# An urgency rank in the planner, recurrences recorded ahead of the heads, the norm factor in the rotary tables, and softmax and projection work moved from VectorE to ScalarE

## Chip, cores and metric

One core of a Trainium2 chip runs the whole program in one launch. The metric is the device time in microseconds (us) of that core, the median of repeated runs; lower is better. The engines are TensorE (PE), VectorE (DVE), ScalarE (ACT), GpSimd (POOL), and SyncE (SP), which issues the transfers.

## The reference

Two transformer blocks follow each other on 512 latent tokens of width 1024, in fp32. The first also has 256 context tokens. Cut to what matters:

```python
# block 1: swiglu FFN, then token mixing (retention and gated linear attention, "GLA"), then swiglu FFN
x = x + 0.5 * m_l[2] * swiglu(modulate(rms_norm(x)), ffn1_w1, ffn1_w3, ffn1_w2)   # ctx likewise
x = x + m_l[5] * token_mixing(modulate(rms_norm(x)), modulate(rms_norm(ctx)), w_in, ...)
x = x + 0.5 * m_l[8] * swiglu(modulate(rms_norm(x)), ffn2_w1, ffn2_w3, ffn2_w2)
# block 2
xn = rmsnorm(h, norm_mix_g)
q, k, v, u, y = split(xn @ w_in_2)               # 512 columns each
q, k = rope(q, positions), rope(k, positions)
attn = dilated_mixture_attention(q, k, v)        # 8 heads of 64, mixture over three dilations
uc = centred_depthwise_conv(u, conv_w, conv_b)
rec = bidirectional_rglru(uc, ...) * gelu(y)     # r, i = sigmoid(...); linear recurrence, both ways
h = h + concatenate([attn, rec]) @ w_out_2
h = h + memory_cross_attention(rmsnorm(h), rmsnorm(mem), ...)
h = h + square(relu(rmsnorm(h) @ w_mlp_in)) @ w_mlp_out
return rmsnorm(h, norm_final_g)
```

## The kernel before

Activations lie feature-major, as tiles of 128 features by 512 tokens. Each fp32 factor is split into a high and a low part in fp32r (`pair`, `split`; weights in `wload`: `wh` is made by ScalarE, `wl` by VectorE), and a product is three matmuls: high by high, low by high, high by low. A sum of products lies in one of the 8 PSUM banks (tag `ps`; tiles `p` for projections, `as`, `at`, `ao` in attention). `MOST` limits how many banks some kinds may hold at a time, so `as` and `at` have two each.

The program records every operation with `Engine` and `Plan.add`. `Plan.issue()` then decides the order on each engine: it walks a model of time with a cost for each operation, and from the operations whose inputs are ready it takes the one that can start first. Among those that can start at the same moment it takes the one that was recorded first (`pick`). On VectorE and ScalarE an operation that was recorded earlier is also taken if it would start a little later (`YIELD`); on ScalarE `pick` stays with the activation table that is loaded, up to a limit. Each engine then runs its list strictly in that order. All operations are recorded through one helper, so the profile gives them all one line, L365, and the tiles' names tell them apart.

The change touches mainly block 2's mixer, at 1380 to 1640 us:

- `heads(i)` projects q and k of two heads, scales them (`fac` is `mix1`, the norm factor), rotates them (`rotated`: `sw` is a copy with swapped rows, by a transfer, then three VectorE operations with the tables `pcos` and `psin`), and splits them (`aqh`, `aql`, `akh`, `akl`).
- `attend(hp)` is the attention of these two heads, as 8 rows (2 heads by 4 tiles `i` of 128 queries). In each row the scores `as` come from two matmuls, VectorE adds the log counts and takes the extreme (`asm`, `mx`), ScalarE takes the exponential with its sum (`dn`), VectorE takes the reciprocal and scales the row, PE transposes it in four pieces (`at`), and ScalarE copies it out (`pt`). Then 64 matmuls of half a tile make `ao`.
- `convolve(i)` makes `uc`, `recur(i, j)` the recurrence for two tiles of it in both directions (all `rg_` tiles, chains on VectorE), and `gated(i)` the gate: `gy` is the y projection scaled by `fac`, then its gelu, then times `rec`.
- The projection `w2_out` sums over attention outputs and gated recurrences (`mix[0..7]`). It is the last user of all of them.

In token mixing (block 1), GpSimd makes some `lo` halves and copies of 64x64 pieces (`pg<-pd`) for GLA. `go` is a sum of GLA outputs on PE, `ro` one of retention.

Of the kernel before, what the change touches and what calls it, by code (L numbers as in the profile page):

```python
# [2 lines left out]

# [36 lines left out]
GROWN = 3  # L40

MOST = {"as": 2, "at": 2, "gl": 2, "gs": 2, "gx": 2, "rs": 2, "cs": 2, "ctp": 2, "rgr": 2, "rgi": 2}
LEVELS = (1, 2, 4, 8, 16, 32)

VEC = {}
# [99 lines left out]
class Plan:  # L145
# [9 lines left out]
    YIELD = 0.3  # L155

    def __init__(self, tc):
        self.tc, self.ops, self.caps, self.warm = tc, [], {}, False

    def engine(self, name, engine):  # L160
        return Engine(self, name, engine)
# [42 lines left out]
    def cost(self, name, method, args, kwargs, outs, ins):  # L204
        def cols(x):
            return int(np.prod(x.shape[1:]))

        if name == "PE":
            n = cols(args[0])
            rhs = args[2] if method == "matmul" else args[1]  # L210
            if method == "matmul" and rhs.tile.dtype == F32R and n >= 256:
                self.warm = True
                return 0.422 * n
            part = 1 if args[0].shape[0] != 64 else 0.75 if n == 64 else 0.53
            if method == "transpose":
                part = 0.5
            return part * max(1.69 * n * (1 if self.warm else 2), 213.0 if n < 64 else 107.0)
        if name == "SP":
            x = outs[0] if outs else ins[0]
            return int(np.prod(x.shape)) * 4 / 360.0 + 50  # L220
        n = max(cols(x) for x in outs)
        if name == "ACT":
            return 93 + 0.833 * n + 93 * sum(isinstance(kwargs.get(k), View) for k in ("bias", "scale", "accum_out"))
        if name == "POOL":
            return 150 + 2.1 * n
        if method == "reciprocal":
            return 60 + 6.3 * n
        if method == "tensor_tensor_reduce":
            return 330 + 1.04 * n
        pointers = sum(isinstance(x, View) and x.shape == (128, 1) for x in args[1:])  # L230
        fast = method in ("tensor_copy", "tensor_scalar", "memset") and not any(x.tile.key[0] == "pp" for x in ins)
        return 66 + (0.53 if fast else 1.04) * n + 60 * pointers

    def issue(self):
        ops, n = self.ops, len(self.ops)
# [26 lines left out]
        left = {t: t.left for t in seen}  # L262
        ahead = {}
        oldest, done = 0, [False] * n
        start, best, stale = [0.0] * n, {}, set(engines)
        order = []

# [17 lines left out]
        def pick(e):  # L285
            t0, choice = None, None
            cand = []
            for i in avail[e]:
                if i > oldest + self.WINDOW:
                    continue  # L290
                w = allowed(i)
                if w is not None:
                    cand.append((max(ready[i], w, clock[e]), i))
            if not cand:
                return None
            first = min(c[0] for c in cand)
            if e in ("DVE", "ACT"):

                i = min(c[1] for c in cand if c[0] <= first + 1.0)
                soon = [c for c in cand if c[1] < i and c[0] - first <= self.YIELD * ops[i][7]]  # L300
                if soon:
                    first = min(soon, key=lambda c: c[1])[0]
            now = [c for c in cand if c[0] <= first + 1.0]
            if e == "ACT":
                stay = [c for c in now if ops[c[1]][8] is None or table in ops[c[1]][8]]
                old = min(now, key=lambda c: c[1])
                if stay and not (first - ready[old[1]] > self.PATIENCE):
                    now = stay
            c = min(now, key=lambda c: c[1])
            return c  # L310

        while oldest < n:
# [65 lines left out]
def tile_two_blocks(ctx: ExitStack, tc: tile.TileContext, a: dict, out: bass.AP, dbg=None):  # L378
# [94 lines left out]
    def wwide(ap):  # L473

        return wcols(wload(ap[:, :1024]), 4, 256) + wcols(wload(ap[:, 1024:]), 4, 256)
# [407 lines left out]
        dump(f"c1_{k}", ctx_.x[k])  # L883


    hl_, hc_ = lat.h, ctx_.h


# [15 lines left out]
    def fm(ap, with_ctx, evac):  # L904

        w = wcols(wload(ap))
        ps = [bank()] + ([bank()[:, :NC]] if with_ctx else [])
        if leading[0] > 0:
            leading[0] -= 1
            two = [ps[0], bank()]  # L910
            for i, span in enumerate(((0, 256), (256, 512))):
                gemm([two[i][:, :256]], w, [cutp(lat.h, *span)])
                evac(slice(*span), two[i][:, :256])
            if with_ctx:
                gemm([ps[1]], w, [ctx_.h])
                evac(None, ps[1])
            return
        gemm(ps, w, [lat.h] + ([ctx_.h] if with_ctx else []))
        evac(slice(0, 512), ps[0])
        if with_ctx:  # L920
            evac(None, ps[1])
# [443 lines left out]
    V.tensor_scalar(ang, ang, lim, -lim, op0=ALU.min, op1=ALU.max)  # L1365
    S_.activation(pcos, n_, AF.Sin)
    S_.activation(psin, ang, AF.Sin)
    V.tensor_scalar(psin, psin, sgn, None, op0=ALU.mult)


    aq, ak = [None] * 4, [None] * 4
# [6 lines left out]
    def heads(i):  # L1378


        def parts(w, scale, name):
            x, hi, lo = slot(name + "t"), slotr(name + "h"), slotr(name + "l")
            fm(w, False, lambda _, pl: V.scalar_tensor_tensor(x, pl, scale, mix1, op0=ALU.mult, op1=ALU.mult))
            rotated(x, x, pcos, psin)
            S_.activation(hi, x, AF.Copy)
            V.tensor_sub(lo, x, hi.bitcast(F32))
            return hi, slotr(name + "s"), lo

        h0, h1, lo = parts(a["w2_q"][i], 0.125, "aq")
        sync.dma_start(h1[high].bitcast(F32), h0[high].bitcast(F32))  # L1390
        sync.dma_start(h1[low].bitcast(F32), lo[high].bitcast(F32))
        sync.dma_start(h0[high].bitcast(F32), lo[low].bitcast(F32))
        aq[i] = h0, h1
        h0, h1, lo = parts(a["w2_k"][i], 1.0, "ak")
        sync.dma_start(h1[high].bitcast(F32), h0[high].bitcast(F32))
        for one, two in ((h0, h1), (lo, slotr("akm"))):
            if one is lo:
                sync.dma_start(two[high].bitcast(F32), one[high].bitcast(F32))
            sync.dma_start(two[low].bitcast(F32), one[high].bitcast(F32))
            sync.dma_start(one[high].bitcast(F32), one[low].bitcast(F32))  # L1400
        ak[i] = (h0, h1), (lo, two)

    heads(0)
    for u in range(2):
        w = wwide(a["w2_v"][u])
        for t in range(4):
            po = bank()[:, :256]
            tok_major(w, lat.h, t, po)
            S_.activation(av[t][:, u * 256 : (u + 1) * 256], po, AF.Copy, scale=mixf[:, t : t + 1])


    sp8, sp4 = small(8, "sp8"), small(8, "sp4")
# [22 lines left out]
    def attend(hp):  # L1435
        pt = []
        for hh in range(2):
            for i in range(4):
                ps = bank("as")
                q, (k, lo) = aq[hp][hh][:, i * P : (i + 1) * P], ak[hp]  # L1440
                T.matmul(ps, q, k[hh], start=True, stop=False)
                T.matmul(ps, q, lo[hh], start=False, stop=True)
                sm = slot("asm")
                mx = plan.tile(tp, [P, 1], F32, "mx", fresh("mx"), 4)
                dn = plan.tile(tp, [P, 1], F32, "dn", fresh("dn"), 4)

                V.tensor_tensor_reduce(sm, ps, lnc[i], -1.0, 3.0e38, ALU.add, ALU.min, accum_out=mx)
                S_.activation(sm, sm, AF.Exp, scale=-1.0, bias=mx, accum_out=dn)
                V.reciprocal(dn, dn)
                V.tensor_scalar(sm, sm, dn, None, op0=ALU.mult)  # L1450
                pq = bank("at")
                for j in range(4):
                    T.transpose(pq[:, j * P : (j + 1) * P], sm[:, j * P : (j + 1) * P], ident)
                pt.append(slot("pt"))
                S_.activation(pt[-1], pq, AF.Copy)
        po = bank("ao")
        for i in range(4):
            for j in range(4):
                for hh in range(2):
                    h = 2 * hp + hh  # L1460
                    T.matmul(po[64 * hh : 64 * hh + 64, i * P : (i + 1) * P], av[j][:, h * 64 : h * 64 + 64],
                             pt[4 * hh + i][:, j * P : (j + 1) * P], start=(j == 0), stop=(j == 3))
        o = slot("aov")
        S_.activation(o, po, AF.Copy)
        dump(f"attn_{hp}", o)
        mix[hp] = pair(o)
# [40 lines left out]
    def gated(i):  # L1507
# [4 lines left out]
        dump(f"rec_{i}", gy)  # L1512
        mix[4 + i] = pair(gy)

    convolve(0)
    convolve(1)
    recur(0, 1)
    heads(1)  # L1520
    attend(0)
    heads(2)
    convolve(2)
    convolve(3)
    attend(1)
    recur(2, 3)
    gated(0)
    gated(1)
    heads(3)
    attend(2)  # L1530
    gated(2)
    gated(3)
    attend(3)
    lat.x = xt = [slot("x") for _ in range(NK)]
    for k in range(NK):
# [237 lines left out]
```

## Time and profile before

| | before |
|---|---|
| median of 3 runs | 2069.81 us (2064.95 to 2073.78) |
| the profiled execution | 2069.04 us, span 2067.3 us |
| mean granted TensorE clock | 0.984 |
| busy in the span | PE 1991.3 us, DVE 1203.4, ACT 795.1, POOL 49.3 |

The span is the time from the first to the last instruction; the rest of an execution's time lies around it. PE's idle time is 76 us, the difference between span and busy time.

### The profile page before, as it was taken

To read this page: it belongs to the slowest core of one execution; us is meant where nothing else is said; L and a number is where in the kernel's file an instruction comes from. 1 tells how busy PE (TensorE), PEld (TensorE's weight loads), DVE (VectorE), ACT (ScalarE), POOL (GpSimd) and SP (SyncE) were. 2 spreads that over 40 slices of the span, in tenths; PEclk is the share of its full clock that TensorE was granted. 3 is DMA by queue.
4 is the path that set the end of the run, shared out by engine and by line. 5 is a ranking of instruction groups with operands and counts; after the bars stand their busy time and mean duration, and the time that the engine had idled before them with its cause. 6 is when DMAs were issued, how large, how long until landed. Compare 5 with 4: busy or idle time off the path is not lost.

```text
span 2067.3 us, 27811 instructions
## 1 busy us (share of the span) xinstructions
PE 1991.3 (96%) x11033; PEld 1686.7 (82%) x11033; DVE 1203.4 (58%) x2221; ACT 795.1 (38%) x1239; POOL 49.3 (2%) x62
## 2 busy tenths in 40 slices
PE   5899999999999998999999999999987999999998
PEld 4879888888888876988988888888765888888887
DVE  7887844426247777589733333376977575343344
ACT  6452121221225654365332222245666463233241
POOL 0000000000000023110000000000000000000000
PEclk9989999999999999999999999999998999999999
DMA  8876624416132112232233333235242214333321
GB/s 314 274 234 199 198 76 137 147 63 218 58 107 88 53 52 72 67 92 75 85 117 92 119 93 103 83 102 161 57 137 55 62 52 135 100 94 100 94 70 41
DMA packets 76801, 231.33 MB, mean 112 GB/s; under 512 B 9808, under 2 KB 12544, under 8 KB 76672
## 3 DMA queue, kind: packets, MB, share of 16 engines
q1 hardware_dynamic: 76672, 229.57, 35.4%
q8 instruction: 86, 1.41, 0.3%
q14 instruction: 43, 0.35, 0.1%
HBM read 212.10 MB, written 7.34 MB: 106 GB/s over the span
## 4 chain that ended last, share of the span: by engine, by line
PE 90%; DVE 5%; ACT 2%; DMA 2%; issue 1%; POOL 0%; SPq 0%; DVEq 0%; ACTq 0%; POOLq 0%
PE p L365 81%; PE gs L365 1%; PE ro L365 1%; PE rs L365 1%; PE at L365 1%; PE st L365 1%; PE go L365 1%; DVE junk L365 1%; DMA wr<-in_ffn_up_dram 1%; PE ao L365 1%; PE gl L365 1%; PE as L365 1%; PE rb L365 0%; DVE rg_r L365 0%; PE co L365 0%
## 5 line engine op out<-in xcount | busy, mean ns | idle before, releaser
L365 ACT ACTIVATE wh<-wr 128x1024 fp32r<-128x1024 f32 (+4 forms) x295 | 298.1, 1013 | 751.8 <-PE p L365 581.0
L365 PE MATMUL p<-hh,wh 128*128 128x512 f32 (+1 forms) x1320 | 505.9, 390 | 12.8 <-ACT hh L365 7.3
L365 PE MATMUL p<-hl,wh 128*128 128x512 f32 (+1 forms) x1320 | 508.3, 389 | 0.0
L365 DVE TENSOR_TENSOR wl<-wr,wh 128x1024 fp32r<-128x1024 f32 (+4 forms) x295 | 343.0, 1168 | 168.6 <-ACT wh L365 78.1
L365 PE MATMUL p<-hh,wl 128*128 128x512 f32 (+1 forms) x1320 | 362.2, 387 | 3.9 <-DVE wl L365 3.9
L365 PE MATMUL p<-hi,wh 128*128 128x512 f32 (+1 forms) x831 | 307.3, 377 | 9.7 <-DVE gy L365 9.7
L365 PE MATMUL p<-lo,wh 128*128 128x512 f32 (+1 forms) x831 | 308.1, 377 | 0.0
L365 PEld LDWEIGHTS p<-hh,wh 128*128 128x128 f32 x1320 | 249.7, 190 | 55.9 <-ACT hh L365 9.3
L365 PEld LDWEIGHTS p<-hh,wl 128*128 128x128 f32 x1320 | 243.9, 190 | 52.6 <-DVE wl L365 4.3
L365 PEld LDWEIGHTS p<-hl,wh 128*128 128x128 f32 x1320 | 251.7, 191 | 37.4 <-issue 0.7
L365 PE MATMUL p<-hi,wl 128*128 128x512 f32 (+1 forms) x831 | 216.0, 376 | 0.0
L365 PEld LDWEIGHTS p<-hi,wh 128*128 128x128 f32 x831 | 156.9, 189 | 32.9 <-DVE gy L365 10.1
L365 PEld LDWEIGHTS p<-lo,wh 128*128 128x128 f32 x831 | 157.4, 189 | 21.1 <-issue 0.2
L365 PEld LDWEIGHTS p<-hi,wl 128*128 128x128 f32 x831 | 149.4, 189 | 27.6 <-issue 0.3
L365 PEld LDWEIGHTS p<-h,wh 128*128 128x128 f32 x816 | 138.8, 189 | 26.1
L365 DVE CUSTOM_DVE_ANT_0 junk<-wr,cond,vec 128x1024 f32<-128x1024 f32 x112 | 143.3, 1280 | 21.6 <-DMA wr<-in_ada_w_dram 20.8
L365 PE MATMUL p<-h,wh 128*128 128x256 f32 x816 | 145.5, 280 | 0.0
L365 DVE TENSOR_TENSOR act<-act,p 128x512 f32<-128x512 f32 (+1 forms) x68 | 38.3, 583 | 177.6 <-PE p L365 176.2
L365 DVE SCALAR_TENSOR_TENSOR x<-p,gate,x 128x512 f32<-128x512 f32 (+1 forms) x59 | 42.6, 723 | 106.2 <-PE p L365 106.1
L365 DVE TENSOR_TENSOR x<-p,x 128x512 f32<-128x512 f32 (+1 forms) x51 | 33.6, 659 | 115.8 <-PE p L365 115.7
L365 PE MATMUL p<-h,wl 128*128 128x256 f32 x408 | 97.3, 279 | 0.0
L365 PEld LDWEIGHTS p<-hid,wh 128*128 128x128 f32 x352 | 64.3, 188 | 14.3
(344 smaller groups left out, 2367.4 us busy)
## 6 DMA issues: line engine op xcount, KB each, us to landing
wr<-in_ffn_up_dram SPq DMA_DIRECT2D x100, 512.0 KB, 3.7
wr<-in_ada_w_dram SPq DMA_DIRECT2D x88, 512.0 KB, 4.4
wr<-in_mlp_up_dram SPq DMA_DIRECT2D x32, 512.0 KB, 3.6
wr<-in_mlp_dn_dram SPq DMA_DIRECT2D x32, 512.0 KB, 3.5
wr<-in_w_out_dram SPq DMA_DIRECT2D x16, 512.0 KB, 3.7
wr<-in_ffn_dn_dram SPq DMA_DIRECT2D x16, 448.0 KB, 3.2
wr<-in_ffn_dn_dram SPq DMA_DIRECT2D x16, 384.0 KB, 3.2
wr<-in_ffn_dn_dram SPq DMA_DIRECT2D x16, 320.0 KB, 2.9
```

The costliest lines, as they stand in the source:

```text
L365: ins = getattr(engine, method)(*args, **kwargs).ins
```

## The change

`Plan.issue` gets a rank. The new `latest` schedules the recorded operations backwards from the end of the program, and the later an operation may begin in that schedule, the later its rank. Operations recorded ahead of `plan.mark`, which stands between the first FFN and token mixing, keep their record order. `pick` uses the rank wherever it used the record index. The planner's cost of a fp32r matmul changes from 0.422n to 13 + 0.418n ns.

In block 2, the two recurrences are recorded ahead of most of the heads, and the V projections (`values`) behind `heads(0)` and `convolve(3)`. The factor `mix1` is multiplied into `pcos` and `psin` once. The eight evacuations of q and k, which multiplied by it on VectorE, become ScalarE copies with a constant scale. In `attend`, the rows with even `i` (16 of 32) are scaled by ScalarE.

```diff
 MOST = {"as": 2, "at": 2, ...}
+LOOK = 12
...
             if method == "matmul" and rhs.tile.dtype == F32R and n >= 256:
-                return 0.422 * n
+                return 13 + 0.418 * n
...
+    def latest(self, after):
+        ops, n = self.ops, len(self.ops)
+        left = [len(x) for x in after]
+        engines = sorted({o[0] for o in ops})
+        clock, heaps, begin = dict.fromkeys(engines, 0.0), {e: [] for e in engines}, [0.0] * n
+        due = [0.0] * n
...
+        for _ in range(n):
+            best = None
+            for e in engines:
+                near = heapq.nsmallest(LOOK, heaps[e])
+                for j in near:
+                    at = max(clock[e], due[-j])
+                    if best is None or (at, j) < best[:2]:
+                        best = at, j, e
...
+            name, cost = ops[i][0], ops[i][7]
+            clock[e] = begin[i] = at + cost
+            for d in ops[i][5]:
+                f = ops[d][0]
+                hop = (0 if f in ("SP", "PE") else self.CHAIN) if f == name else self.HOPS.get((f, name), self.HOP)
+                due[d] = max(due[d], begin[i] + hop + (2000 if f == "SP" else 0))
...
+        return [(0, i) if i < self.mark else (1, -x) for i, x in enumerate(begin)]
...
-            c = min(now, key=lambda c: c[1])
+            c = min(now, key=lambda c: rank[c[1]])
...
+    plan.mark = len(plan.ops)
     hl_, hc_ = lat.h, ctx_.h
...
-    V.tensor_scalar(psin, psin, sgn, None, op0=ALU.mult)
+    V.scalar_tensor_tensor(psin, psin, sgn, mix1, op0=ALU.mult, op1=ALU.mult)
+    V.tensor_mul(pcos, pcos, mix1)
...
-            fm(w, False, lambda _, pl: V.scalar_tensor_tensor(x, pl, scale, mix1, op0=ALU.mult, op1=ALU.mult))
+            fm(w, False, lambda _, pl: S_.activation(x, pl, AF.Copy, scale=scale))
...
-                V.tensor_scalar(sm, sm, dn, None, op0=ALU.mult)
+                if i % 2:
+                    V.tensor_scalar(sm, sm, dn, None, op0=ALU.mult)
+                else:
+                    S_.activation(sm, sm, AF.Copy, scale=dn)
...
     convolve(0)
     convolve(1)
     recur(0, 1)
+    convolve(2)
+    heads(0)
+    convolve(3)
+    values()
+    recur(2, 3)
     heads(1)
     attend(0)
-    heads(2)
-    convolve(2)
-    convolve(3)
-    attend(1)
-    recur(2, 3)
     gated(0)
     gated(1)
+    heads(2)
+    attend(1)
+    gated(2)
+    gated(3)
     heads(3)
     attend(2)
-    gated(2)
-    gated(3)
     attend(3)
```

(The old record began with `heads(0)` and the V projections, ahead of `convolve(0)`.)

The rank moves instructions on every engine behind the first FFN. Three places follow. The first is VectorE in the mixer at the end of `recur(2, 3)`, where the gate's evacuations (`gy<-p`), those of `heads(3)` (`aqt`, `akt`) and the first row of `attend(2)` (ISA, `as_2474`) stand. Before:

```order
L365 SCALAR_TENSOR_TENSOR rg_r_2430_13380<-rg_a_2432_13495,rg_r_2430_13380 128x512
L365 TENSOR_TENSOR rg_i_2431_13389<-rg_i_2431_13389,rg_r_2430_13380 128x512
L365 SCALAR_TENSOR_TENSOR rg_r_2430_13380<-rg_a_2432_13495,rg_i_2431_13389 128x512
L365 TENSOR_TENSOR rg_r_2425_13368<-rg_r_2425_13368,rg_r_2430_13380 128x512
L365 TENSOR_TENSOR gy_2441_13622<-p_2445_13003,fac_2139_12218 128x512
L365 TENSOR_TENSOR gy_2448_13624<-p_2452_13202,fac_2139_12218 128x512
L365 SCALAR_TENSOR_TENSOR aqt_2455_13631<-p_2461_13402,fac_2139_12218 128x512
L365 SCALAR_TENSOR_TENSOR akt_2464_13635<-p_2470_13475,fac_2139_12218 128x512
L365 ISA asm_2475_13643,mx_2476_13644<-as_2474_13517,lnc_2154_8621 128x512
```

In the changed kernel the end of `recur(2, 3)` stands behind `attend(0)`, between weight halves and the first gate's evacuation, and ahead of `attend(1)`'s second row; `aqt` and `akt` are on ScalarE.

```order
L403 SCALAR_TENSOR_TENSOR rg_a_2285_13143<-rg_u_2296_13168,rg_a_2285_13143 128x512
L403 SCALAR_TENSOR_TENSOR rg_u_2298_13204<-rg_r_2288_13012,rg_s_2297_13177 128x512
L403 SCALAR_TENSOR_TENSOR rg_r_2283_13005<-rg_a_2285_13143,rg_r_2283_13005 128x512
L403 TENSOR_TENSOR rg_i_2284_12961<-rg_i_2284_12961,rg_r_2283_13005 128x512
L403 TENSOR_TENSOR wl_2458_13227<-wr_2456_12703,wh_2457_13213 128x1024
L403 SCALAR_TENSOR_TENSOR rg_a_2290_13165<-rg_u_2298_13204,rg_a_2290_13165 128x512
L403 ISA asm_2404_13248,mx_2405_13249<-as_2403_13242,lnc_2154_8680 128x512
L403 ISA asm_2410_13256,mx_2411_13257<-as_2409_13251,lnc_2155_8678 128x512
L403 TENSOR_TENSOR gy_2370_13267<-p_2374_12990,fac_2139_12210 128x512
```

The unbroken chain of recurrence rows became single rows among others, the gate's evacuation no longer follows the last of them, and no evacuation of q or k is left on VectorE.

The second place is the rotation of `heads(3)` on VectorE, in `attend(2)`. Before, it stands ahead of the reciprocals and scalings of two rows (`dn_2495`, `dn_2501`):

```order
L365 TENSOR_TENSOR sw_2462_13638<-sw_2462_13638,psin_2149_8926 128x512
L365 TENSOR_TENSOR aqt_2455_13631<-aqt_2455_13631,pcos_2148_8977 128x512
L365 TENSOR_TENSOR aqt_2455_13631<-sw_2462_13638,aqt_2455_13631 128x512
L365 TENSOR_TENSOR sw_2471_13647<-sw_2471_13647,psin_2149_8926 128x512
L365 TENSOR_TENSOR akt_2464_13635<-akt_2464_13635,pcos_2148_8977 128x512
L365 TENSOR_TENSOR aql_2457_13751<-aqt_2455_13631,aqh_2456_13746 128x512
L365 TENSOR_TENSOR akt_2464_13635<-sw_2471_13647,akt_2464_13635 128x512
L365 RECIPROCAL dn_2495_13725<-dn_2495_13725 128x1
L365 RECIPROCAL dn_2501_13736<-dn_2501_13736 128x1
L365 TENSOR_SCALAR asm_2493_13707<-asm_2493_13707,dn_2495_13725 128x512
```

In the changed kernel it stands ahead of the scalings too, but at the first rows of `attend(2)` (`asm_2495` is the second), with a row's ISA between its two halves:

```order
L403 TENSOR_TENSOR aqt_2469_13450<-aqt_2469_13450,pcos_2148_9090 128x512
L403 TENSOR_TENSOR aqt_2469_13450<-sw_2476_13542,aqt_2469_13450 128x512
L403 ISA asm_2495_13664,mx_2496_13665<-as_2494_13565,lnc_2155_8678 128x512
L403 ISA mx_2496_13665 128x1
L403 TENSOR_TENSOR sw_2485_13581<-sw_2485_13581,psin_2149_9064 128x512
L403 TENSOR_TENSOR akt_2478_13533<-akt_2478_13533,pcos_2148_9090 128x512
L403 TENSOR_TENSOR akt_2478_13533<-sw_2485_13581,akt_2478_13533 128x512
L403 ISA asm_2501_13693,mx_2502_13694<-as_2500_13612,lnc_2156_8687 128x512
```

The rotation moved from the fifth row of the attention to the first ones, and its halves are no longer one block.

The third place is GpSimd in token mixing, between the two pairs of GLA heads (`pg_1123` to `pg_1130` belong to the first, `pg_1233` to `pg_1240` to the second; `rkc`, `rk`, `rq` are retention's). Before:

```order
L365 TENSOR_TENSOR lo_1198_7121<-pg_1130_6598,hi_1197_7109 128x512
L365 TENSOR_TENSOR lo_1360_7516<-rkc_1329_7261,hi_1359_7447 128x512
L365 TENSOR_TENSOR lo_1341_7541<-rk_1325_7524,hi_1340_7532 128x512
L365 TENSOR_TENSOR lo_1349_7571<-rq_1321_7546,hi_1348_7559 128x512
L365 COPY pg_1233_7127<-pd_1244_7018 64x64
L365 COPY pg_1234_7133<-pd_1244_7018 64x64
```

After:

```order
L403 TENSOR_TENSOR lo_1198_7021<-pg_1130_6545,hi_1197_7012 128x512
L403 COPY pg_1234_7066<-pd_1244_6912 64x64
L403 COPY pg_1233_7062<-pd_1244_6912 64x64
L403 COPY pg_1234_7066<-pd_1244_6912 64x64
L403 COPY pg_1233_7062<-pd_1244_6912 64x64
L403 COPY pg_1236_7089<-pd_1244_6912 64x64
```

The three retention halves ahead of the second pair's copies moved behind all of them.

## Rows read from the trace of the kernel before

**Rows 1.** The page: the chain that ended last, by engine.
```profile
PE 90%; DVE 5%; ACT 2%; DMA 2%; issue 1%; POOL 0%; SPq 0%; DVEq 0%; ACTq 0%; POOLq 0%
```

**Rows 2.** Windows by stage: stretch, length, busy PE, PEld, DVE, ACT, POOL, clock.
```profile
950.00:1380.00 430.00, 430.00 (x2107) 364.81 (x2106) 200.01 (x353) 143.44 (x195) 0.00 (x0) 1.00 0.32 100
...
1450.00:1500.00 50.00, 47.63 (x254) 35.82 (x253) 45.01 (x89) 30.17 (x52) 0.00 (x0) 1.00 0.22 52
1500.00:1550.00 50.00, 42.75 (x233) 33.28 (x231) 39.91 (x65) 31.00 (x48) 0.00 (x0) 0.94 0.45 137
1550.00:1600.00 50.00, 38.81 (x245) 28.98 (x247) 37.95 (x92) 33.82 (x65) 0.00 (x0) 0.85 0.22 56
...
1700.00:2050.00 350.00, 350.00 (x1612) 292.51 (x1611) 150.62 (x203) 113.22 (x144) 0.00 (x0) 1.00 0.29 88
```

**Rows 3.** PE's waits in the mixer's end, 1553 to 1610 us: total, times, longest.
```profile
PE p L365 <- DVE gy L365: 9.7, 1, 9.7
PE at L365 <- ACT akh L365: 4.4, 1, 4.4
PE as L365 <- ACT pt L365: 1.6, 2, 0.9
```

**Rows 4.** VectorE's timeline at the end of the first long wait.
```profile
1552.22 1.28 DVE L365 TENSOR_TENSOR gy<-p,fac 128x512 f32<-128x512 f32 x2
```

**Rows 5.** PE's timeline right after that wait.
```profile
1553.55 0.63 PE L365 MATMUL p<-lo,wh 128*128 128x512 f32 x1
1553.98 0.63 PE L365 MATMUL p<-hi,wl 128*128 128x512 f32 x1
```

**Rows 6.** VectorE's timeline around the second long wait.
```profile
1565.02 0.69 DVE L365 TENSOR_TENSOR sw<-sw,psin 128x512 f32<-128x512 f32 x1
...
1569.55 0.88 DVE L365 TENSOR_SCALAR asm<-asm,dn 128x512 f32<-128x512 f32 x2
```

**Rows 7.** Windows around the two long waits, and of the last two attentions.
```profile
1547.00:1558.00 11.00, 5.04 (x12) 3.98 (x13) 10.69 (x20) 6.95 (x11) 0.00 (x0) 0.53 0.10 25
1568.00:1575.00 7.00, 4.13 (x16) 2.92 (x18) 5.25 (x15) 3.11 (x6) 0.00 (x0) 0.51 0.56 128
...
1553.00:1604.00 51.00, 42.76 (x277) 31.99 (x278) 35.61 (x89) 35.23 (x67) 0.00 (x0) 0.89 0.22 55
```

**Rows 8.** PE's timeline late in the last attention.
```profile
1591.87 1.03 PE L365 MATMUL at<-ident,asm 128*128 128x128 f32 x8
1592.66 0.47 PE L365 MATMUL p<-lo,wh 128*128 128x512 f32 x1
1592.97 0.39 PE L365 MATMUL as<-aks,aqs 128*128 128x512 f32 x1
1593.19 0.39 PE L365 MATMUL as<-akm,aqs 128*128 128x512 f32 x1
...
1593.98 1.31 PE L365 MATMUL ao<-pt,av 128*64 128x128 f32 x18
1595.22 0.50 PE L365 MATMUL p<-hi,wl 128*128 128x512 f32 x1
```

**Rows 9.** ScalarE's groups in the mixer, 1380 to 1640 us: count, busy us, mean ns.
```profile
L365 ACT ACTIVATE asm<-asm,mx 128x512 f32<-128x512 f32 x32 | 22.9, 716 | 1.8 <-DVE mx L365 1.7
L365 ACT ACT_TABLE_LOAD x17 | 21.8, 1283 | 0.3
L365 ACT ACTIVATE pt<-at 128x512 f32<-128x512 f32 x32 | 18.8, 594 | 20.1 <-PE at L365 19.9
L365 ACT ACTIVATION_READ_ACCUMULATOR asm<-asm,mx 128x1 f32 x32 | 6.1, 189 | 0.0
```

**Rows 10.** VectorE's scaling of the rows in the same stretch.
```profile
L365 DVE TENSOR_SCALAR asm<-asm,dn 128x512 f32<-128x512 f32 x32 | 15.4, 486 | 1.0
```

**Rows 11.** Windows of GLA in token mixing.
```profile
750.00:800.00 50.00, 47.37 (x380) 33.43 (x379) 33.90 (x74) 26.62 (x47) 12.36 (x20) 0.97 0.21 55
800.00:850.00 50.00, 43.49 (x282) 35.52 (x281) 38.46 (x46) 22.02 (x35) 24.52 (x28) 1.00 0.27 73
```

More of the change, by code (lines that the diff above doesn't have):

```diff
@@ L1 @@
+import heapq
 import math
@@ L157, in __init__ @@
     def __init__(self, tc):
-        self.tc, self.ops, self.caps, self.warm = tc, [], {}, False
+        self.tc, self.ops, self.caps, self.warm, self.mark = tc, [], {}, False, 0
     def engine(self, name, engine):
@@ L232, in cost @@
         return 66 + (0.53 if fast else 1.04) * n + 60 * pointers
+    def latest(self, after):
[4 more added lines that the diff above has]
+        due = [0.0] * n
+        for i in range(n):
+            if left[i] == 0:
+                heapq.heappush(heaps[ops[i][0]], -i)
+        for _ in range(n):
[6 more added lines that the diff above has]
+                        best = at, j, e
+            at, j, e = best
+            heaps[e].remove(j)
+            heapq.heapify(heaps[e])
+            i = -j
+            name, cost = ops[i][0], ops[i][7]
[4 more added lines that the diff above has]
+                due[d] = max(due[d], begin[i] + hop + (2000 if f == "SP" else 0))
+                left[d] -= 1
+                if left[d] == 0:
+                    heapq.heappush(heaps[f], -d)
+        return [(0, i) if i < self.mark else (1, -x) for i, x in enumerate(begin)]
     def issue(self):
@@ L264, in issue @@
         oldest, done = 0, [False] * n
+        rank = self.latest(after)
         start, best, stale = [0.0] * n, {}, set(engines)
@@ L297, in pick @@
             if e in ("DVE", "ACT"):
-                i = min(c[1] for c in cand if c[0] <= first + 1.0)
-                soon = [c for c in cand if c[1] < i and c[0] - first <= self.YIELD * ops[i][7]]
+                i = min((c[1] for c in cand if c[0] <= first + 1.0), key=rank.__getitem__)
+                soon = [c for c in cand if rank[c[1]] < rank[i] and c[0] - first <= self.YIELD * ops[i][7]]
                 if soon:
-                    first = min(soon, key=lambda c: c[1])[0]
+                    first = min(soon, key=lambda c: rank[c[1]])[0]
             now = [c for c in cand if c[0] <= first + 1.0]
@@ L305, in pick @@
                 stay = [c for c in now if ops[c[1]][8] is None or table in ops[c[1]][8]]
-                old = min(now, key=lambda c: c[1])
+                old = min(now, key=lambda c: rank[c[1]])
                 if stay and not (first - ready[old[1]] > self.PATIENCE):
                     now = stay
-            c = min(now, key=lambda c: c[1])
+            c = min(now, key=lambda c: rank[c[1]])
             return c
@@ L1401, in heads @@
         ak[i] = (h0, h1), (lo, two)
[L1403 to L1409, printed above, removed]
     sp8, sp4 = small(8, "sp8"), small(8, "sp4")
@@ L1513, in gated, with values @@
         mix[4 + i] = pair(gy)
+    def values():
+        for u in range(2):
+            w = wwide(a["w2_v"][u])
+            for t in range(4):
+                po = bank()[:, :256]
+                tok_major(w, lat.h, t, po)
+                S_.activation(av[t][:, u * 256 : (u + 1) * 256], po, AF.Copy, scale=mixf[:, t : t + 1])
     convolve(0)
```

## The prediction

> **What bounds it now.** The chain of the run that ended last comes first: 90% of it is PE [rows 1]. The sum to make is therefore of PE: its idle time, 76 us of a span of 2067.3, and any stretch at the lower clock. Next come windows by stage. In the stages between GLA and the mixer, and in the MLP, PE is busy without a gap (430.00 of 430, 350.00 of 350): whatever order the rank gives there, there is no idle time to win [rows 2]. The mixer's end is another matter. From 1450 to 1600 PE works 47.63, 42.75 and 38.81 of 50 us each, so it is idle for 20.8 us, and the granted clock falls to 0.94 and 0.85. VectorE works 122.9 of these 150 us and ScalarE 95.0 [rows 2].
>
> The waits by releaser then say on whom PE waits. Two single waits make up most of the 20.8 us: 9.7 us for `gy` from VectorE, and 4.4 us for rows of `attend(2)`, put down to `akh` [rows 3]. VectorE's timeline explains the first. The gate's y projections were finished and held PSUM banks, but their evacuations stand in VectorE's list behind the unbroken end of `recur(2, 3)`. They ran at 1552.22, and PE went on at once [rows 4]. The order of before, shown above, has just this sequence. The second wait is the rotation of `heads(3)`: it begins at 1565.02, ahead of the scalings, and the two scalings for which the transposes waited come at 1569.55 [rows 6]. ScalarE's `akh` is only the neighbour that ended last.
>
> Behind each wait the clock is at its half level, 1.2 GHz: windows around them show 0.53 and 0.51 [rows 7]. Projection matmuls there begin 0.43 us apart [rows 5], and 0.22 us apart at full clock [rows 8].
>
> **The change, part by part.**
>
> *Recurrences recorded earlier, and the rank.* The changed order has the end of `recur(2, 3)` in single rows between softmax rows and weights, before the gate's evacuations and ahead of most of `attend(1)`. No chain of about 20 us of VectorE work then stands between a finished y projection and its bank. I take the whole wait: 9.7 us. It stays partly if those rows push softmax rows of `attend(0)` back, which I price below.
>
> *Rotation of `heads(3)`.* It still precedes some scalings, but at the first rows of `attend(2)`, while y projections are left for PE to do: the changed order has 64 projection matmuls between the first scores of `attend(2)` and the last `ao`. At 0.22 us these are 14 us of cover. I take 4.4 us. With the cover gone it would cost the same again.
>
> *Clock.* Behind the two waits PE worked 5.04 and 4.13 us [rows 7] at about half speed. At full clock that work takes 0.22/0.43 of it, so 4.5 us are saved at most. Some of these instructions are transposes that wait in between, so I take 4.2. Sum of gains: 9.7 + 4.4 + 4.2 = 18.3 us.
>
> *Evacuation and half the scaling on ScalarE.* In the mixer VectorE loses 16 scalings of 0.486 us [rows 10] and 8 evacuations, taken at the 0.69 of an operation of the same size [rows 6]: 13.3 us. It gains one table operation. ScalarE gains 8 copies of 0.594, like `pt`, and 16 scalings. These have no row: a copy is 0.594 and an exponential with a per-partition operand 0.716 [rows 9], and I take 0.72, the form that is nearer. The changed order also has 22 table loads where there were 17. That is 4.8 + 11.5 + 5 × 1.283 = 22.7 us more on ScalarE.
>
> Is that hidden? I count the last two attentions, from the first scores of `attend(2)` on. ScalarE in the changed order: 16 exponentials with their sums at 0.80 (0.716 and 0.189, which overlap a little), 16 `pt` at 0.594, 8 scalings at 0.72, 3 loads at 1.283, 12 other copies at about 0.6, and one weight half of about 1.1: 12.8 + 9.5 + 5.8 + 3.8 + 7.2 + 1.1 = 40.2 us. PE there: 32 score matmuls at 0.22, 64 transposes (eight begin in 0.79), 128 `ao` (18 in 1.24) and 64 projection matmuls at 0.22 [rows 8]: 7.0 + 6.3 + 8.8 + 14.1 = 36.2 us. In the order of before the same count gives ScalarE 34.6 (no scalings, 4 loads, no weight half) and PE 43.2 (96 projection matmuls). So ScalarE, with a spare of 9 us, becomes the longer by 4 us. Before, with that spare, PE still lost 51.00 − 42.76 − 4.4 = 3.8 us in these rows [rows 7], mostly behind `pt` [rows 3]. I put the new loss at 4 us above this. The ends: nothing, if ScalarE starts early enough, and 10 us, if each of the 8 scalings also waits behind an exponential (8 × 0.80) and the 4 us remain.
>
> In `attend(0)` and `attend(1)` more loads stand between rows, since square roots and tanh of the recurrences alternate with exponentials. Two of the five new loads take 2.6 us. I take 2 us, with 0 and 6.4 (all five) as ends.
>
> The Trainium skill ("ScalarE: Activation LUTs", What ACT_TABLE_LOAD costs) gives a switch of table about 1.28 us and as much as 1.38 us of drain on top, and advises doing all of one set before switching, which speaks against this order. In this trace 17 loads take 1283 ns each with 0.3 us of idle time ahead of all of them [rows 9]: the first figure agrees, and no drain is seen as a gap. With the drain the five loads would take 6.9 us more, and the sum would give 2064 in place of 2057; the row speaks so plainly that I give it no chance of its own.
>
> *The tables' norm factor.* One VectorE operation more, and one somewhat longer, once, in a stretch where both tables are long ready: nothing. If they came late they would cost 0.7 us.
>
> *The planner's matmul cost.* It issues nothing. For 512 columns it says 227 in place of 216 ns, near the 0.22 measured, and shifts neighbours only where PE has work: nothing.
>
> *The rank in token mixing.* GpSimd's copies for the second GLA pair now precede three halves for retention. In 800 to 850 PE is idle for 6.5 us, in 750 to 800 for 2.6 [rows 11]. The copies come earlier, but retention products that filled PE beside GLA come later too. The gain is at most the 6.5, and the loss about twice the 2.6, if the second pair is left as bare as the first and the first becomes barer. Between a gain of 6.5 and a loss of 5, I take 0.
>
> **Sum.** 18.3 − 4 − 2 = 12.3 us. The profiled execution took 2069.04 us, 0.8 below the median of the runs, so the profiled execution should take 2056.7, and the median about 2057.
>
> **The rivals.**
>
> *All of it is covered.* ScalarE's work fits between PE's, and the smaller waits go as well: 18.3 + 3.8 + 2.4 (the idle time of 1450 to 1500) and about 2 in token mixing make 26.5, so 2043. For it: VectorE and ScalarE would be about even, near 110 and 118 of 150 us. Against it: the row's chain runs through ScalarE three times where it was twice.
>
> *The wait only moves.* The recurrence rows still have to pass VectorE, now among the softmax rows of `attend(0)`, whose transposes would wait for them. If the 9.7 us come back there, 2066.5. For it: VectorE is 80% busy in this stretch. Against it: rows come singly, with projections around them.
>
> *ScalarE takes VectorE's place, and it gets slower.* In each of 16 rows the scaling waits behind an exponential that stands ahead of it: 0.72 − 0.49 + 0.80 = 1.03 us, and five loads lie bare: 16.5 + 6.4 = 22.9 against 18.3, so about 2074. The point from which it decides: 18.3 − 6.4 = 11.9, so from 12 rows of the 16 on. Projections beside the rows speak against that many.
>
> *Token mixing loses its fillers.* The mixer gains 12.3, GLA loses 5: 2062.
>
> **How the numbers follow.** Forecast (2051 to 2063) 0.50; all covered (2040 to 2050) 0.14; GLA loses 0.12; the wait moves 0.14; ScalarE takes over 0.10. Faster by over 0.5%, which is about what a measurement can tell and means below 2059.5, takes three quarters of the forecast, the covered case and a little of GLA: 0.54. ScalarE's case passes 2080 only if GLA's loss or part of the moved wait joins it, for which I take half of its weight: slower 0.05. The rest, 0.41, is within 0.5%. The range 2044 to 2070 leaves out the better half of the covered case and most of the last one.
>
> **What would show it.** Right: no PE wait for `gy` over 2 us, none for `akh` over 1, PE idle from the mixer's start to its end near 13 us in place of 21, and the waits left are for `asm` or `pt` from ScalarE in the last two attentions. Wrong: a long wait of a transpose for `asm` in `attend(0)`, idle time of PE over 14 us in GLA's 750 to 850, where it was 9.1, or a clock below 1 in attention stretches.

## The result, and the profile after

The changed kernel takes 2049.35 us (median of 4 runs, 2041.94 to 2052.36), the kernel before 2070.4 beside it. The ratio is 0.9895, with a 95% interval of 0.9861 to 0.993: faster by 21 us, where 12.8 were forecast, inside the range. The profiled execution took 2052.36 us with a span of 2050.6.

The windows by stage of the changed kernel, with the columns of [rows 2]:

```profile
0.00:150.00 150.00, 116.96 (x583) 99.27 (x584) 120.19 (x241) 75.94 (x123) 0.70 (x6) 0.90 0.81 271
750.00:800.00 50.00, 46.58 (x350) 31.99 (x350) 37.03 (x77) 25.86 (x46) 10.81 (x18) 0.93 0.16 48
800.00:850.00 50.00, 48.18 (x269) 38.62 (x269) 28.93 (x38) 22.15 (x33) 18.49 (x25) 1.00 0.27 77
1450.00:1500.00 50.00, 50.00 (x315) 40.86 (x313) 41.67 (x76) 41.47 (x68) 0.00 (x0) 1.00 0.49 142
1500.00:1550.00 50.00, 48.58 (x276) 39.50 (x273) 38.62 (x73) 40.93 (x65) 0.00 (x0) 1.00 0.54 143
1550.00:1600.00 50.00, 49.77 (x328) 39.19 (x327) 30.84 (x74) 38.43 (x74) 0.00 (x0) 1.00 0.22 61
1535.00:1581.00 46.00, 44.66 (x343) 34.90 (x341) 28.41 (x76) 40.60 (x79) 0.00 (x0) 1.00 0.35 96
690.00:800.00 110.00, 104.73 (x845) 77.17 (x845) 83.52 (x194) 52.09 (x96) 11.89 (x20) 0.88 0.15 43
```

From 1450 to 1600 PE is idle for 1.7 us, where it was 20.8 [rows 2], and the clock stays at 1.00. VectorE's work there fell from 122.9 to 111.1 us and ScalarE's rose from 95.0 to 120.8, much as summed. In GLA, 750 to 850, PE is idle for 5.2 us where it was 9.1 [rows 11]. But from 690 to 800 the clock is 0.88; in the kernel before the same stretch reads 0.98:

```profile
690.00:800.00 110.00, 106.35 (x904) 80.66 (x904) 82.62 (x209) 55.26 (x100) 12.37 (x20) 0.98 0.21 60
```

PE's waits of the mixer in the changed kernel, 1370 to 1640, with the columns of [rows 3], are one line:

```profile
PE as L403 <- DMA akl<-akl: 1.4, 2, 1.1
```

Nothing waits for `gy`, for rows that a rotation delays, or for ScalarE. ScalarE's groups there, with the columns of [rows 9]:

```profile
L403 ACT ACT_TABLE_LOAD x23 | 29.5, 1283 | 0.4
...
L403 ACT ACTIVATE asm<-asm,dn 128x512 f32<-128x512 f32 x16 | 11.2, 716 | 1.4 <-DVE dn L403 1.3
...
L403 ACT ACTIVATE aqt<-p 128x512 f32<-128x512 f32 x4 | 2.3, 585 | 0.0
```

A scaling on ScalarE takes 716 ns, an evacuation 585: 0.72 and 0.594 us were taken. The 23 loads include the one at the start of cross attention, so the mixer has 22, where the kernel before had 17.

One reading of the change has to be set right. The end of `recur(2, 3)` does not stand ahead of all gate evacuations. VectorE's timeline has the first evacuation ahead of the last five recurrence rows:

```profile
1509.64 0.69 DVE L403 TENSOR_TENSOR gy<-p,fac 128x512 f32<-128x512 f32 x1 [0.22 <-PE p L403]
...
1521.01 0.69 DVE L403 SCALAR_TENSOR_TENSOR rg_r<-rg_a,rg_r 128x512 f32<-128x512 f32 x1
...
1525.45 0.69 DVE L403 TENSOR_TENSOR rg_r<-rg_r,rg_r 128x512 f32<-128x512 f32 x1
```

A sum puts the two effects side by side. Take PE's idle time of an execution, and PE's busy time inside the stretches where the clock's record shows 1.2 GHz. Half of the latter is lost time, since intervals there are about doubled [rows 5, 8]. Span less idle time less that half should be the same work for every order. It is so within 9 us: 1965 to 1973 us in all fourteen profiles of this study. Smaller differences are below what this sum can tell.

| profile | span | idle | busy at half clock | work | mixer: idle, half clock | token mixing: idle, half clock |
|---|---|---|---|---|---|---|
| before | 2067.3 | 76.0 | 43.8 | 1969.4 | 20.8, 19.2 | 12.7, 3.1 |
| changed | 2050.6 | 54.9 | 53.8 | 1968.7 | 2.0, 3.4 | 8.9, 27.1 |

("Mixer" is 970 to 1640 us, "token mixing" 600 to 970.) In these two executions the mixer gave 18.8 + 7.9 = 26.7 us. Token mixing gave 3.8 us of idle time and took 12.0 through the clock. The first 150 us took 2.9 and the tail gave 0.6.

### The profile page after: what moved, and what is told of

The parts are those of the page before. It is cut to its first block, busy times and chain, and to the rows that moved or that the text cites. A ratio compares the mean times of both kernels' runs of the same rounds, so it can differ in the third digit from the quotient of the medians.

```text
span 2050.6 us, 27788 instructions
## 1 busy us (share of the span) xinstructions
PE 1995.6 (97%) x11033; PEld 1690.0 (82%) x11033; DVE 1182.5 (58%) x2198; ACT 812.9 (40%) x1267; POOL 47.8 (2%) x62
## 4 chain that ended last, share of the span: by engine, by line
PE 89%; DVE 4%; DMA 3%; ACT 2%; POOL 1%; issue 1%; POOLq 0%; SPq 0%; DVEq 0%; ACTq 0%
PE p L403 80%; PE gs L403 1%; DMA wr<-in_ffn_up_dram 1%; PE ro L403 1%; PE rs L403 1%; PE ao L403 1%; POOL lo L403 1%; PE st L403 1%; PE go L403 1%; PE gx L403 1%; PE as L403 1%; DVE junk L403 1%; PE at L403 1%; DMA akl<-akl 0%; PE rb L403 0%
## 5 line engine op out<-in xcount | busy, mean ns | idle before, releaser
L403 DVE TENSOR_TENSOR act<-act,p 128x512 f32<-128x512 f32 (+1 forms) x68 | 38.2, 582 | 121.3 <-PE p L403 121.2
L403 ACT ACTIVATE ss<-x 128x256 f32<-128x256 f32 (+1 forms) x80 | 38.3, 500 | 78.3 <-DVE x L403 77.9
L403 PEld LDWEIGHTS p<-h,wl 128*128 128x128 f32 x408 | 68.7, 189 | 0.1
```

Of the source, the lines that this page charges most:

```text
L403: ins = getattr(engine, method)(*args, **kwargs).ins
```

## Experiments

Each ran beside the kernel before. The runs lie on three chips, and the kernel before took 2072.6, 2073.4 and 2074.3 us on them, so kernels are compared by their ratios to it, which stand here with 95% intervals. The changed kernel is at 0.9895 [0.9861, 0.993].

**The record order undone.**

```diff
-    convolve(2); heads(0); convolve(3); values(); recur(2, 3); heads(1); attend(0); ...
+    (the calls of the kernel before, heads(0) and the V projections first)
```

> The changed kernel with the old record order of the mixer; rank, ScalarE moves and cost stay. Theory 1 (the gain is the early recurrences): a long wait of PE for gy or a transpose comes back in the mixer and the time is 2062 to 2070. Theory 2 (the gain is VectorE's relief by ScalarE): at most 4 us slower than the changed kernel, 2049 to 2054. Theory 3 (the gain is the rank, which puts recurrences early whatever the record says): the same as the changed kernel, 2046 to 2052.

2045.75 us, 0.9876 [0.9859, 0.9894]: as fast as the changed kernel. PE's longest wait in the mixer is 0.8 us. Theory 1, which the prediction had taken together with the rank, falls. Here all four gate evacuations stand together behind recurrence rows, as late as in the kernel before, but PE does not wait for them: from 1540 to 1557 us it works on rows of `attend(2)`, with projections between them. The longest wait, and the evacuations:

```profile
PE p L403 <- DVE lo L403: 0.8, 1, 0.8
```

```profile
1556.62 2.47 DVE L403 TENSOR_TENSOR gy<-p,fac 128x512 f32<-128x512 f32 x4
```

**The rank undone.**

```diff
-        return [(0, i) if i < self.mark else (1, -x) for i, x in enumerate(begin)]
+        return list(range(n))
```

> The changed kernel with the record index in place of the rank everywhere. Theory 1: the record order alone puts the recurrences early, so 2049 to 2055. Theory 2: the same. Theory 3 (the rank): the long waits return at least in part, 2060 to 2070.

2075.31 us, 1.0022 [1.0005, 1.0039], slower than any of the three theories had it: nothing is left of the gain, although recurrences are recorded early and ScalarE has its share. PE's waits from 960 to 1600 us:

```profile
PE p L403 <- DVE ub L403: 9.0, 1, 9.0
PE p L403 <- DVE wl L403: 4.2, 1, 4.2
PE at L403 <- ACT asm L403: 1.9, 1, 1.9
PE at L403 <- ACT pt L403: 1.5, 3, 1.0
```

The wait of 9.7 us for `gy` [rows 3] became one of 9.0 for `ub`, the evacuation of a convolution's projection, that now stands behind the early recurrences. This is the rival in which the wait only moves, and it happens without the rank.

**The ScalarE moves undone.**

```diff
-    V.scalar_tensor_tensor(psin, psin, sgn, mix1, op0=ALU.mult, op1=ALU.mult)
-    V.tensor_mul(pcos, pcos, mix1)
+    V.tensor_scalar(psin, psin, sgn, None, op0=ALU.mult)
...
-            fm(w, False, lambda _, pl: S_.activation(x, pl, AF.Copy, scale=scale))
+            fm(w, False, lambda _, pl: V.scalar_tensor_tensor(x, pl, scale, mix1, op0=ALU.mult, op1=ALU.mult))
...
-                if i % 2:
-                    V.tensor_scalar(sm, sm, dn, None, op0=ALU.mult)
-                else:
-                    S_.activation(sm, sm, AF.Copy, scale=dn)
+                V.tensor_scalar(sm, sm, dn, None, op0=ALU.mult)
```

> The changed kernel with q and k evacuated and all rows scaled on VectorE again, and the tables without the norm factor; record order, rank and cost stay. Theory 1: VectorE has 13 us more in the mixer but the order hides most of it, 2049 to 2055. Theory 2: PE waits for VectorE's asm and the time is 2058 to 2066.

2055.13 us, 0.9911 [0.9891, 0.9932], which overlaps the changed kernel. PE's idle time from 970 to 1640 is 6.2 us against 2.0 (2.8 of it for `mx`). If these moves are worth anything here, it is some 3 us by the ratios; the intervals don't settle it. With the old record order they are worth about 1 us, less than the intervals can tell: 0.9876 with them, above, and 0.9883 without, below.

**The old matmul cost.**

```diff
-                return 13 + 0.418 * n
+                return 0.422 * n
```

> The changed kernel with the planner's old matmul cost. In the profiles, PE lost about 3 us more in the first 150 us after the change (waits for wh and wl 14.5 against 8.7), ahead of the point where the rank begins, so only the cost can have moved it. If that is the order's doing, 3 us faster than the changed kernel, about 2046, with waits for wh and wl near 9; if it is scatter of the transfers between runs, the same time and these waits near 9 to 15.

2066.89 us, 0.9969 [0.9955, 0.9983]: about 15 us slower than the changed kernel, which neither case foresaw. The first 150 us are not the place: PE's idle time there is 33.4 us against 33.0, so what the changed kernel lost there was no doing of the cost. The place is below.

**Parts alone.** Rank and cost without the rest; the cost alone; the rank alone with the old cost (all three with the old record order and all work on VectorE); and the changed kernel with the mark moved, so that the rank begins with block 2's mixer:

```diff
-    plan.mark = len(plan.ops)          # ahead of token mixing
...
+    plan.mark = len(plan.ops)          # ahead of block 2's rotary tables
```

> The kernel before with the rank and the new matmul cost only: old record order, q and k and all rows on VectorE. If the rank does the work and the cost must go with it, most of the gain is here: 2050 to 2058, without a wait above 3 us in the mixer, and 3 to 6 us slower than the changed kernel with the old record order. If the ScalarE moves or the record order are needed for it, 2060 to 2070.

> The kernel before with the new matmul cost only. If the cost alone places instructions better, 2058 to 2065. If it only matters together with the rank, within 0.3% of before, 2065 to 2077, with the long wait for gy or one of its size in the mixer.

> The kernel before with the rank only: old cost, old record order, no ScalarE moves. If the cost is needed with the rank, 2064 to 2075, with token mixing starting and ending later than in the changed kernel by 7 to 14 us, as in the run with the old cost. If that run's loss came from its record order, 2050 to 2058.

> The changed kernel with the mark moved to the start of block 2's mixer, so token mixing and the second FFN keep record order among ready operations. The rank's part in the mixer alone: if the gain is all in the mixer, the same as the changed kernel, 2046 to 2052. If the rank also gains in token mixing, 3 to 8 us slower than it, with PE idle there as before (about 12 us from 600 to 950).

| kernel | median us | ratio |
|---|---|---|
| rank and cost alone | 2048.34 | 0.9883 [0.9861, 0.9904] |
| cost alone | 2076.04 | 1.0012 [0.9996, 1.0029] |
| rank alone | 2062.08 | 0.9944 [0.9924, 0.9965] |
| rank from block 2 on | 2048.99 | 0.9889 [0.9866, 0.9912] |

Rank and cost are the whole gain. Together they are faster than expected, and level with the run of the old record order, where 3 to 6 us more were expected. The cost alone keeps the waits (5.7 for `gy` and 4.4 for `akh`). The rank alone has half of the gain, and lies between its two expected cases. With the rank from block 2 on, the view of PE's waits between 970 and 1620 is empty, and the time is the same. That does not mean that the rank does nothing in token mixing. In the profiled execution PE is idle there for 12.4 us, 3.5 more than in the changed kernel's, but busy at half clock for 13.2 us in place of 27.1, which is worth 7 the other way.

**Which use of the cost.** The new one in the forward walk only, then in the rank only:

```diff
+    def older(self, o):                # 0.422 * n for the same matmuls, else o[7]
...
-            name, cost = ops[i][0], ops[i][7]                  # in latest
+            name, cost = ops[i][0], self.older(ops[i])         # first run; the second does this in the walk
```

> The changed kernel with the new matmul cost in the forward walk and the old one in the rank. If the accuracy of the walk's clock matters, as fast as the changed kernel, 2045 to 2052. If it is the rank that needs it, 2058 to 2068, with long half-clock stretches in token mixing.

> The other half: the old cost in the forward walk, the new one in the rank. If the walk needs the new cost, 2058 to 2068, with first GLA scores near 700 us and about 40 us or 20 us at half clock in token mixing; if the rank needs it, 2045 to 2052.

In the walk only: 2065.13 us, 0.9963 [0.995, 0.9975]. In the rank only: 2049.9 us, 0.9885 [0.9868, 0.9903]. The rank needs the new cost, the walk does not. The window from 690 to 800 us of the first, and then of the second:

```profile
690.00:800.00 110.00, 105.09 (x718) 76.64 (x718) 67.73 (x153) 43.50 (x80) 12.54 (x20) 0.75 0.16 46
```

```profile
690.00:800.00 110.00, 107.61 (x834) 80.34 (x832) 79.90 (x187) 52.80 (x96) 11.67 (x20) 0.88 0.18 50
```

PE is busy for 105 and 108 us in both, but the first starts 718 matmuls and the second 834. The loss is clock, not waiting: PE's busy time at half clock in token mixing is 64.2 us in the walk-only run, and 34.0 and 44.4 in the two runs with the old cost in both places, against 27.1 in the changed kernel and 13.7 in rank and cost alone. Their idle time there differs by 3 us at most. Half of 64.2 less 27.1 is 18.6, more than the 16 us between the two kernels' medians.

These are single profiles, and one order can show quite different amounts (last section). The mean clock of every run is firmer. It is 0.974 to 0.982 in all 28 runs of the three kernels whose rank used the old cost, and 0.983 to 0.987 in all 19 of the changed kernel, the old record order, rank and cost alone, and the new cost in the rank only (without the ScalarE moves, 0.982 to 0.990). A run's span times its mean clock leaves out what the clock took. Its medians are 2014 to 2020 us in the first three kernels and 2015 to 2018 in the other four: nearly all of the difference is clock. That it falls in token mixing rests on the profiles.

**A higher cost.**

```diff
-                return 13 + 0.418 * n
+                return 26 + 0.418 * n
```

> The changed kernel with 26 + 0.418n as the planner's matmul cost, 240 ns for 512 columns where 227 is near what runs show. If what matters is a cost near the real one, slower than the changed kernel, 2052 to 2065. If a higher cost only gives slack that helps, 2040 to 2049, which would be a version that beats both.

2064.21 us, 0.9956 [0.9941, 0.9972]. At full clock, projection matmuls of 512 columns begin 227 ns apart in the trace of the changed kernel, which is its planner's cost. A cost above that interval, 240, loses as one below it, 216, does, but by waits more than by the clock, which is 0.981 to 0.986 over the six runs. PE is idle for 16.7 us in token mixing against 8.9 in the changed kernel, and for 6.7 against 2.0 in the mixer; the first 150 us had 5.4 less. Idle time and clock together explain 9.2 of the 13.7 us between the spans; the rest stays open.

**All rows on ScalarE.**

```diff
-                if i % 2:
-                    V.tensor_scalar(sm, sm, dn, None, op0=ALU.mult)
-                else:
-                    S_.activation(sm, sm, AF.Copy, scale=dn)
+                S_.activation(sm, sm, AF.Copy, scale=dn)
```

> The changed kernel with all 32 probability rows scaled on ScalarE. In the changed kernel's last two attentions PE worked 44.7 of 46 us and ScalarE 40.6; eight more scalings at 0.716 make ScalarE 46.3. If ScalarE had only these 4 us of room, waits of PE for asm or pt appear, 2 to 6 us slower than the changed kernel, 2051 to 2056. If the planner finds room elsewhere, the same, 2046 to 2052.

2056.02 us, 0.9918 [0.9903, 0.9934], some 5 us above the changed kernel by the ratios, with overlapping intervals. PE's waits of the mixer now name ScalarE and the rows:

```profile
PE at L403 <- ACT pt L403: 3.5, 2, 3.3
PE as L403 <- DVE mx L403: 2.1, 1, 2.1
PE at L403 <- DVE mx L403: 1.0, 2, 0.6
```

PE's idle time from 970 to 1640 is 7.6 us against 2.0. So in these profiles there is room for the 16 scalings that the change moved and not for 16 more. No version here is shown to beat the changed kernel: the old record order, rank and cost alone, and the rank from block 2 on are level with it.

## Why the prediction came out as it did

**The two long waits** (9.7 and 4.4 us) went, as forecast, and with them the half clock behind them. The size was right, the cause only in part. The prediction credited the wait for `gy` to the recurrences recorded earlier and the rank together. The old record order is as fast, and the new one without the rank has a wait of 9.0 us in place of 9.7. So it is the rank alone that removes it, and not by one detail of the order. In the changed kernel evacuations go in between recurrence rows. With the old record order they still stand behind them, and PE has attention rows to do meanwhile.

**The clock in the mixer** was put at 4.2 us, for the stretches behind the two waits. All half-clock stretches of the mixer count: 19.2 us of busy time became 3.4, worth 7.9.

**ScalarE as the longer engine**, minus 4 us, is the term that was most mis-sized. The prediction set ScalarE's 40.2 us against 36.2 of PE. The window from 1535 to 1581 us, first scores of `attend(2)` to the last `ao`, shows ScalarE at 40.60 and PE at 44.66. PE still had 46 `ao` and 8 transposes of `attend(1)` to do there, about 4 us at the prediction's own prices, which the count left out. The other 4.5 us are prices that were too low, most of all the scores: 32 of them hold PE for 9.6 us until the next matmul begins, where 7.0 were taken. PE was the longer engine by 4 us, and the 1.3 us of idle time left are fewer than the 3.8 that the prediction had kept from before. Together this term was off by 6.5 us. That the margin is small is what the run with all rows on ScalarE suggests.

**The first two attentions**, minus 2 us, cost nothing: from their first scores, at 1474 us, to those of `attend(2)`, at 1535, PE is idle for 0.3 us, and the 2.4 us of 1450 to 1500 in the kernel before went too. The Trainium skill ("ScalarE: Activation LUTs", Table sets: the hidden batching unit) advises doing all the work of one table set together. Here five loads more lay beside PE's work, at 1283 ns each with 0.4 us of idle time ahead of all 23, so the trace again shows no drain as a gap.

In sum the mixer did what the rival "all of it is covered" says (24.5 us there), and a little more by the clock: 26.7. Of the signs that the prediction named, the waits for `gy` and `akh` went, but idle time fell to 2.0 us, not 13, and no wait for ScalarE is left.

**Token mixing** was put at 0, between 6.5 and −5. Its idle time gave 3.8 us, inside the bounds. What the prediction did not have is its clock: 12.0 us lost in the profiled execution, 5.3 in that of rank and cost alone (13.7 us at half against 3.1 before). These two ran the same list in this stage (last section), so the loss is known as a spread and not as one size.

**The planner's cost** was put at nothing, because it issues nothing and PE always had work. That step was wrong. With the rank, the old cost makes the kernel slower by 0.7%, and only its use in the rank does so. Shown is where the time goes, the half clock in token mixing, most of it in GLA. Which of the order's details lowers the clock there was not separated.

**The sum** was 12.3 us of gain against 21 between the medians, and 16.7 between the two profiled spans (the changed kernel's is the slowest of its four runs). Between the spans the mixer gave 14.4 us more than the sum had for it, while token mixing took 8.2 and the first 150 us 2.9, for both of which the sum had nothing. The range held because these misses have opposite signs; that is luck.

## What to carry to other kernels

Before an engine is called the longer one in a stretch, count all of its work between the same two moments, what is left of the stage before included; a margin of a few us can have the other sign. When a scheduler gets a new priority, test the priority and the record order apart: here the hand-made order was worth nothing once the rank was there, and a rank worked out with matmul costs 5% below the measured interval, or 6% above, lost more than half of its gain. Account for a span as work, plus idle time, plus half of the busy time at half clock: the last two trade against each other, and waits alone would not have found the second. To tell what an order does to the clock, take the mean clock of all runs; one profile can mislead.

## What the runs showed of the hardware

One list of instructions can get different amounts of half clock. By the names and shapes in the traces, the lists of PE, VectorE, ScalarE and GpSimd from the start to the end of GLA are the same in five kernels: the changed one, the old record order, without the ScalarE moves, rank and cost alone, and all rows on ScalarE. Yet busy time at half clock in token mixing is 27.1, 27.0, 13.7, 13.7 and 20.5 us, and the time from the first `gs` to the end of the last `go` of GLA is 124.3, 124.3, 118.1, 118.2 and 121.3 us. The three kernels without a rank in token mixing but with the new cost (no rank, the cost alone, the rank from block 2 on) share another list, with 26.9, 37.5 and 13.2 us at half clock. The window from 690 to 800 us of rank and cost alone, beside 0.88 in the changed kernel:

```profile
690.00:800.00 110.00, 104.72 (x926) 78.44 (x925) 87.13 (x203) 53.95 (x100) 13.47 (x28) 0.94 0.17 50
```

Runs of one and the same kernel differ too: the changed kernel's fastest (2041.94 us) has a mean clock of 0.987, the other three (2048 to 2052) 0.983 to 0.984, and without the ScalarE moves 2045.63 us goes with 0.990 and 2058.99 with 0.982. What decides it was not found.
